# A 64-byte gap in front of the normalised activations, and a wider ring for one small tile

## The chip, the cores and the metric

The kernel runs on one core of a Trainium2 chip. The metric is the device time of one execution in microseconds, the median of several runs. Engines are called as in the profile: PE is the matrix engine (PEld its weight loads), DVE the vector engine, ACT the scalar engine, POOL the general one, SP the queue that issues most DMAs.

## The reference

Two blocks work one after the other on 512 tokens of 1024 channels in float32.

```
x = x + y @ w_out   # twice; y from hn @ w_in (1024 -> 4096): 8 heads of
                    # chunked attention, 4 heads of retention, silu gates
x = rms_norm(x)
x = x + 0.5 * swiglu(rms_norm(x))      # 1024 -> 2 x 2816 -> 1024
x = x + token_mixer(rms_norm(x))       # 1024 -> 3344 -> 1024: pooling, HGRN,
                                       # RWKV-7, gated linear attention
x = x + 0.5 * swiglu(rms_norm(x))
x = rms_norm(x)
```

Most of the arithmetic is dense products of the normalised x, or of a hidden layer, with a weight matrix.

## The kernel before

x is kept transposed, in eight tiles of 128 channels by 512 tokens. A dense product is taken in units of 128 output columns. For a unit, `wunit` loads 1024 rows by 128 columns of the weight (512 KB) into `wraw`, ACT casts them to float32r (`whi`, L188), and DVE subtracts to get the rest (`wlo`, L189). `proj_cm` then issues, for each of the eight channel tiles k, the three matmuls of `mm3`: z high by whi (L210), z low by whi (L211), z high by wlo (L212). So a unit is 24 matmuls; the stationary operand of each is a 128x128 slice of whi or wlo, the moving operand a whole 128x512 tile, and the result gathers in one bank of PSUM. Each matmul loads a new stationary slice (PEld).

The moving tiles have four names. z (z0h, z0l to z7h, z7l, made by `zsplit`) are the normalised activations, used by the projections of both layers, by the first product of both feed-forward stages, and by the mixer. h (h0h, h0l to h21h, h21l) are the hidden channels of a feed-forward stage (`ffn`): its second product takes 22 of them, 66 matmuls for each of eight output tiles. ys are the gated results of a layer, multiplied by w_out at the end of `layer`. ysh and ysl are the same for the mixer (`mix_out`). In `proj_tm` (the attention and retention values) the roles are swapped: slices of z are stationary, and slices vhi and vlo of the weight, 256 columns, move.

Every engine works through its instructions in the order of the program. Between the units stand the matmuls of attention (L456 to L480), of retention (L493 to L511), and of the mixer's recurrences; the units of the next heads are placed among those of the heads before, and in the mixer an order written out by hand (`MIX_ORDER`) does so.

SBUF is laid out by pools in the order in which they are made: persistent tiles, wp (wraw, whi, wlo, three slots each), sm (small tiles), tmp, xp (x), zp (z), and behind it the pool of the stage: b1 for the layers, ffn for a feed-forward stage, mix for the mixer. Within a pool each tile stands behind the one before, its bytes per partition rounded up to 32. All the large tiles take a multiple of 512 bytes per partition, so what sets a tile's start modulo 512 is the small tiles ahead of it. In the compiled program before, the starts modulo 512 are

```
wraw, whi, wlo            320
x, R, fa, th, z           256
b1: cosT, sinT, g, vhi, vlo                 256
b1: rtm 256 and 288; all made after rtm, ys among them   320
ffn: R and h              256
mix: ysh, ysl              32   (X, b and others 352)
```

A slice of 128 float32 of a weight tile takes 512 bytes, so each slice has the start of its tile modulo 512. The ring `rtm` (two slots of 4 float32 in 32 bytes each, made in the middle of b1) is what puts the tiles made after it 64 bytes further. The program uses SBUF up to byte 229,200 per partition.

Of the kernel before, what the change touches and what calls it, by code (L numbers as in the profile page):

```python
# [8 lines left out]
F32 = mybir.dt.float32  # L9
# [6 lines left out]
PSUM = bass.MemoryType.PSUM  # L16

T = 512
D = 1024
NT = T // 128  # L20
# [92 lines left out]
class Build:  # L113
# [36 lines left out]
    def banks(self, ctx, m, a, b, c):  # L150
        """The banks of PSUM beyond the three of psm: m more for dense products, and three pools for the rest."""
        self.mm_ring = [self.psm] * 3
        if m:
            self.mm_ring += [self.pool("psx", m, PSUM, ctx)] * m
        self.psa, self.psb, self.psc = (self.pool(n, k, PSUM, ctx) for n, k in (("psa", a), ("psb", b), ("psc", c)))
# [14 lines left out]

# [1 line left out]
    def wunit(self, src, nk=ND, dst=None):  # L172
        """128 columns of a weight as float32r high and low parts [128, nk, 128]."""
        nc = self.nc
        raw = self.wp.tile([128, 8, 128], F32, tag="wraw", name="wraw")
        nc.sync.dma_start(out=raw[:, :nk, :], in_=src.rearrange("(k p) n -> p k n", p=128))
        return self.wsplit(raw, nk, dst)
# [15 lines left out]
    def split(self, src, pool=None, tag=None, scale=None, alloc=None):  # L193
        """src (float32) times a per-partition scale, as float32r high and low parts."""
        nc = self.nc
        if alloc is None:
            alloc = lambda part: pool.tile([128, T], F32R, tag=tag + part, name=tag + part)
        hi, lo = alloc("h"), alloc("l")
        if scale is None:
            nc.scalar.copy(hi, src)  # L200
            nc.vector.tensor_tensor(out=lo, in0=src, in1=hi.bitcast(F32), op=ALU.subtract)
        else:
            nc.scalar.activation(out=hi, in_=src, func=AF.Copy, scale=scale)  # L203
            nc.vector.scalar_tensor_tensor(out=lo, in0=src, scalar=scale, in1=hi.bitcast(F32),  # L204
                                           op0=ALU.mult, op1=ALU.subtract)
        return hi, lo
# [7 lines left out]
    def proj_cm(self, src, z, order=range(ND), unit=None, bank=None):  # L214
        """128 columns of a weight, channel-major: [128 channels, tokens]."""
        hi, lo = unit or self.wunit(src)
        ps = self.mm_bank(bank)
        for i, k in enumerate(order):
            self.mm3(ps, hi[:, k, :], lo[:, k, :], z[k][0], z[k][1], i == 0, i == ND - 1)
        return ps  # L220

    def proj_tm(self, w, tt, z):
        """256 columns, token-major: [128 tokens, 256]."""
        ps = self.mm_bank()[:, :256]
        hi, lo = w
        s = slice(tt * 128, (tt + 1) * 128)
        for k in range(ND):
            self.mm3(ps, z[k][0][:, s], z[k][1][:, s], hi[:, k, :], lo[:, k, :], k == 0, k == ND - 1)
        return ps

# [1 line left out]
    def rsqrt(self, m, n, k=""):  # L232
        """m: [128, n] positive normal float32 tile; returns 1/sqrt(m)."""
        nc = self.nc
# [5 lines left out]
                                scalar2=float(0x5F3759DF), op0=ALU.mult, op1=ALU.add)  # L240
        # a step of third order, then one of Newton's
        nc.vector.tensor_tensor(out=t, in0=y, in1=y, op=ALU.mult)
# [8 lines left out]
    def sumsq_add(self, st, src, scale=None, alloc=None):  # L251
        """Adds the squares of one channel tile to the running sum of a norm."""
        nc = self.nc
        if st.get("acc") is None:
            st["acc"] = self.tmp.tile([128, T], F32, tag="nacc", name="nacc", bufs=2)
            dst = st["acc"]
        else:
            dst = alloc() if alloc else self.tmp.tile([128, T], F32, tag="nsq", name="nsq")
        kw = {} if scale is None else {"scale": scale}
        nc.scalar.activation(out=dst, in_=src, func=AF.Square, **kw)  # L260
        if dst is not st["acc"]:
            nc.vector.tensor_tensor(out=st["acc"], in0=st["acc"], in1=dst, op=ALU.add)

    def sum_tok(self, acc, n=NT):
        """Sums over channels: [128 tokens, n] from acc [128 channels, n * 128]."""
        ps = self.psc.tile([128, T], F32, tag="c", name="c")
# [11 lines left out]
    def bcast_tok(self, r, pool, tag):  # L278
        """[128 tokens, NT] to every partition: PSUM [128, T]."""
        nc = self.nc  # L280
# [10 lines left out]

# [1 line left out]
    def tables(self):  # L293
# [35 lines left out]

# [1 line left out]
    def first_block(self):  # L331
# [17 lines left out]
    def layer(self, l):  # L349
        nc = self.nc  # L350
        b1 = self.b1
        z = self.z
        w_in = self.a["w_in"]
        first = {}
# [27 lines left out]
        ahead(0, 1, (self.psa, "a"))  # L382
        rtm = b1.tile([128, NT], F32, tag="rtm", name="rtm", bufs=2)
        nc.vector.tensor_copy(out=rtm, in_=rt)
# [30 lines left out]
        def stacked(q, k):  # L415
            """The two heads apart: high and low part of q on the two halves of the rows, the high part of k on
            both, and the low part of k."""
            qs, ks = [], []
# [21 lines left out]
        def attention(p, q, k, v, g):  # L440
            """Heads 2p and 2p + 1; the result times the gate replaces the gate."""
            po = self.psc.tile([128, T], F32, tag="c", name="po")
# [73 lines left out]
        v = None  # L516
# [35 lines left out]

# [1 line left out]
    def ffn(self, w_in, w_out, first, gain=None):  # L554
# [62 lines left out]
    def last_tile(self, ps):  # L617
        """The last channels of the last residual, their squares, and the sums of all, by groups of tokens."""
        nc = self.nc
# [16 lines left out]

# [1 line left out]
    def mixer(self):  # L638
# [5 lines left out]
        with ExitStack() as ctx:  # L644
# [95 lines left out]
            def silu_of(c0, alloc, name, scale):  # L740
                """scale * silu(column group), channel-major."""
                d = scaled(c0, alloc, name, 0.5 * scale)
# [5 lines left out]
            def tokens(src, alloc, name):  # L748
                """[128 channels, tokens] to [128 tokens, NT, 128 channels]."""
                ps = self.psc.tile([128, NT, 128], F32, tag="c", name="pv")  # L750
# [42 lines left out]
    def mix_out(self, y, xs):  # L793
        """The output product of the mixer in two passes: the channels that are ready first, then the rest."""
        nc, x = self.nc, self.x
# [41 lines left out]
    def rwkv(self, e, c):  # L837
        """Heads 2c and 2c + 1: chunks of 64 tokens, two to a tile of 128."""
        nc = self.nc
# [72 lines left out]
        for tp in range(2):  # L912
# [11 lines left out]
            for h in range(2):  # L924
                for i in range(2):
# [4 lines left out]
                                        in1=mLQ.unsqueeze(1).to_broadcast([128, 2, 128]), op=mult)  # L930
        # inverse of I + L: 16 x 16 diagonal blocks by substitution, one block per partition
        scr = self.dp.tile([8, 8, 16, 16], F32, tag="scr", name="scr", bufs=2)
# [64 lines left out]

        # merges 16 -> 32 -> 64
        pst = mm8(lambda r, v, cc: zt[r, v, :], lambda r, v, cc: idq[cc], "pT")
# [13 lines left out]

        # chunk transfer matrices
        for tp in range(2):
# [35 lines left out]

        # chunk to chunk
        S = t("S", (128, 8, 64))
# [11 lines left out]

        # outputs
        bv = t("bv", (128, 8, 64))
# [43 lines left out]
    def gla_core(self, e, q, k, lf, v, finish):  # L1111
        """Gated linear attention for a pair of heads, chunks of 128 tokens: q, k, lf channel-major,
        v token-major. Within a chunk, the pairs of tokens that part at the same level of halving are
        taken in one product, with decays to and from the last token of the left half."""
        nc = self.nc
# [120 lines left out]
    def to_channels(self, on, g, gain):  # L1236
        """The token-major [128, NT, 128] on, transposed, times gain and gate, into the gate's tile."""
        nc = self.nc
# [55 lines left out]
    def hgrn(self, e):  # L1294
# [3 lines left out]
        V = e["V"]  # L1298
        # lower bounds: softmax over the one layer, cumulated, minus the first
        lb = e["small"]("lb", 2)  # L1300
# [96 lines left out]
    def finish(self):  # L1397
        """The last norm, token-major: the channels of x times their gains are transposed, and the tokens scaled
        on the way out of PSUM."""
        nc = self.nc  # L1400
# [16 lines left out]
    def run(self):  # L1417
        nc = self.nc
        self.setup()
        self.zp = self.pool("zp")  # L1420
        self.dp = self.pool("dp", 1, bass.MemoryType.DRAM)
        self.fg = self.pers.tile([128, 8], F32, name="fg")
# [61 lines left out]
```

## Time and profile before

| | before |
|---|---|
| median of 3 runs | 1720.46 us (1719.25 to 1720.58) |
| the profiled execution, from its first to its last instruction | 1720.4 us |
| PE busy | 1695.1 us, 9648 matmuls |
| DVE busy | 987.0 us |
| ACT busy | 628.9 us |
| mean granted clock of PE | 0.989 |

The profiled execution's span is within 0.1 us of the median, so the span and the time can be read as one. A matmul's recorded duration runs on past the start of the next one, since matmuls are pipelined; what a matmul costs in a dense stretch is the distance from its start to the next one's start.

### The profile page before, as it was taken

Reading aid. Unit: us, or ns where it says so; the run is one execution under the profiler, and the core shown is the slowest. Engines: PE = TensorE matmul, PEld = TensorE weight load, DVE = VectorE, ACT = ScalarE, POOL = GpSimd, SP = SyncE. Lnnn points to the kernel's source line nnn. Section 1 sums busy time; section 2 is a strip of 40 time slices with the busy share of each in tenths; the row PEclk is TensorE's granted clock in tenths of the full one; section 3 lists DMA queues with packets and bytes.
Section 4 is the critical chain, followed back from the end, with each engine's and each line's share of the span. In section 5 each row is a group of like instructions: output and inputs, shape, how many; then the busy total and the mean of one; then the engine's idle time right before and its main releaser. Section 6 shows DMA issues by size and latency. Waiting matters only on the chain.

```text
span 1720.4 us, 24093 instructions
## 1 busy us (share of the span) xinstructions
PE 1695.1 (99%) x9648; PEld 1335.9 (78%) x9648; DVE 987.0 (57%) x1972; ACT 628.9 (37%) x1077; POOL 62.4 (4%) x58
## 2 busy tenths in 40 slices
PE   8999999999999999999999999999989999999998
PEld 6777788777778888888888877777767888888886
DVE  7684756554465675554433377658868654454222
ACT  6553323454332432232222235327435332222221
POOL 0001110000111000000000100000200000000000
PEclk9999999999999999999999999989989999999999
DMA  7221223422122223333333432212013323333331
GB/s 239 83 84 38 81 61 92 135 80 80 38 81 64 76 84 100 93 91 98 95 101 108 124 87 66 54 38 59 24 48 96 114 88 98 99 88 90 101 92 59
DMA packets 270673, 147.33 MB, mean 86 GB/s; under 512 B 10576, under 2 KB 264288, under 8 KB 270560
## 3 DMA queue, kind: packets, MB, share of 16 engines
q1 hardware_dynamic: 265600, 140.40, 28.0%
q0 software_dynamic: 1280, 4.20, 0.8%
q8 instruction: 76, 1.25, 0.3%
q10 hardware_dynamic: 3680, 1.19, 0.3%
q14 instruction: 37, 0.30, 0.1%
HBM read 141.30 MB, written 4.46 MB: 85 GB/s over the span
## 4 chain that ended last, share of the span: by engine, by line
PE 92%; DVE 4%; ACT 2%; DMA 1%; issue 1%; SPq 0%; DVEq 0%; ACTq 0%
PE mm L212 26%; PE mm L211 26%; PE mm L210 26%; PE po L480 2%; PE pt L472 1%; PE s L457 1%; PE po L498 1%; PE s L493 1%; PE s L456 1%; DMA wraw<-in_w_in 1%; PE pO L1084 1%; PE pO L1082 1%; DVE xr L1187 0%; PE po L1231 0%; DVE wlo L189 0%
## 5 line engine op out<-in xcount | busy, mean ns | idle before, releaser
L188 ACT CAST whi<-wraw 128x1024 fp32r<-128x1024 f32 (+2 forms) x244 | 244.7, 1004 | 716.7 <-PE mm L211 496.0
L189 DVE TENSOR_TENSOR wlo<-wraw,whi 128x1024 fp32r<-128x1024 f32 (+2 forms) x244 | 287.1, 1179 | 156.9 <-ACT whi L188 156.3
L593 DVE SCALAR_TENSOR_TENSOR fa<-mm,R 128x512 f32<-128x512 f32 x44 | 30.4, 692 | 114.8 <-PE mm L212 114.8
L589 DVE SCALAR_TENSOR_TENSOR fa<-mm,R 128x512 f32<-128x512 f32 x44 | 30.3, 691 | 96.5 <-PE mm L212 95.3
L210 PE MATMUL mm<-z0h,whi 128*128 128x512 f32 x163 | 68.4, 420 | 6.1 <-ACT z0h L203 5.7
L211 PE MATMUL mm<-z7l,whi 128*128 128x512 f32 x163 | 65.8, 404 | 0.9 <-DVE z7l L204 0.9
L212 PE MATMUL mm<-z0h,wlo 128*128 128x512 f32 x163 | 66.2, 406 | 0.0
L211 PE MATMUL mm<-z0l,whi 128*128 128x512 f32 x163 | 66.2, 406 | 0.0
L210 PE MATMUL mm<-z6h,whi 128*128 128x512 f32 x163 | 66.0, 405 | 0.0
L210 PE MATMUL mm<-z4h,whi 128*128 128x512 f32 x163 | 65.9, 405 | 0.0
L212 PE MATMUL mm<-z6h,wlo 128*128 128x512 f32 x163 | 65.9, 404 | 0.0
L211 PE MATMUL mm<-z3l,whi 128*128 128x512 f32 x163 | 65.8, 403 | 0.0
L210 PE MATMUL mm<-z7h,whi 128*128 128x512 f32 x163 | 65.3, 401 | 0.3 <-ACT z7h L203 0.3
L210 PE MATMUL mm<-z5h,whi 128*128 128x512 f32 x163 | 65.6, 402 | 0.0
L212 PE MATMUL mm<-z3h,wlo 128*128 128x512 f32 x163 | 65.5, 402 | 0.0
L211 PE MATMUL mm<-z5l,whi 128*128 128x512 f32 x163 | 65.5, 402 | 0.0
L211 PE MATMUL mm<-z6l,whi 128*128 128x512 f32 x163 | 65.3, 401 | 0.0
L211 PE MATMUL mm<-z4l,whi 128*128 128x512 f32 x163 | 65.3, 401 | 0.0
L212 PE MATMUL mm<-z4h,wlo 128*128 128x512 f32 x163 | 65.3, 401 | 0.0
L210 PE MATMUL mm<-z2h,whi 128*128 128x512 f32 x163 | 65.3, 400 | 0.0
L211 PE MATMUL mm<-z2l,whi 128*128 128x512 f32 x163 | 65.2, 400 | 0.0
L212 PE MATMUL mm<-z1h,wlo 128*128 128x512 f32 x163 | 65.2, 400 | 0.0
(737 smaller groups left out, 4241.4 us busy)
## 6 DMA issues: line engine op xcount, KB each, us to landing
wraw<-in_w_in SPq DMA_DIRECT2D x90, 512.0 KB, 4.0
wraw<-in_ffn_w_in SPq DMA_DIRECT2D x88, 512.0 KB, 3.7
wraw<-in_ffn_w_out SPq DMA_DIRECT2D x32, 512.0 KB, 3.9
wraw<-in_w_out SPq DMA_DIRECT2D x16, 512.0 KB, 4.2
wraw<-in_ffn_w_out SPq DMA_DIRECT2D x16, 384.0 KB, 3.5
bias<-in_relb SPq DMA_DIRECT2D x16, 256.0 KB, 2.8
x<-in_xT SPq DMA_DIRECT2D x8, 256.0 KB, 5.3
decay<-in_decay SPq DMA_DIRECT2D x8, 256.0 KB, 2.9
```

The costliest lines, as they stand in the source:

```text
L188: nc.scalar.copy(hi[:, ks, :], raw[:, ks, :])
L189: nc.vector.tensor_tensor(out=lo[:, ks, :], in0=raw[:, ks, :], in1=hi[:, ks, :].bitcast(F32), op=ALU.subtract)
L210: mm(out, lhsT=lh, rhs=rh, start=start, stop=False)
L211: mm(out, lhsT=lh, rhs=rl, start=False, stop=False)
L212: mm(out, lhsT=ll, rhs=rh, start=False, stop=stop)
L456: nc.tensor.matmul(ps, lhsT=qt, rhs=k[0][h][:, :n], start=True, stop=False)
L457: nc.tensor.matmul(ps, lhsT=qt[hr], rhs=k[1][hr, :n], start=False, stop=True)
L472: nc.tensor.transpose(pt[:, ks], s[:, ks], self.ident)
L480: nc.tensor.matmul(po[64 * h:64 * h + 64, t * 128:(t + 1) * 128], lhsT=v[:, kt, vc:vc + 64], rhs=pts[h][:, ks], start=(kt == 0), stop=(kt ...
L493: nc.tensor.matmul(ps, lhsT=k[:, kt * 128:(kt + 1) * 128], rhs=q[:, T - n:], start=True, stop=True)
L589: nc.vector.scalar_tensor_tensor(out=a2, in0=pg, scalar=0.5, in1=R, op0=ALU.mult, op1=ALU.mult)
L593: nc.vector.scalar_tensor_tensor(out=a2, in0=pu, scalar=0.5, in1=R, op0=ALU.mult, op1=ALU.mult)
```

## The change

A tile of 128 partitions by 16 float32 (64 bytes per partition) is made as the first tile of zp and set to zero by POOL. It is never read. z and all pools behind it start 64 bytes further. The ring rtm takes tiles of 64 float32 (256 bytes) in place of 4, of which the first four columns are used as before; its two slots take 512 bytes in place of 64. So all tiles of b1 made after rtm stand 512 bytes further, which leaves their starts modulo 512 as they were. Docstrings and comments are dropped without a change of line numbers.

```diff
-        rtm = b1.tile([128, NT], F32, tag="rtm", name="rtm", bufs=2)
+        rtm = b1.tile([128, 64], F32, tag="rtm", name="rtm", bufs=2)[:, :NT]
...
         self.zp = self.pool("zp")
+        gap = self.zp.tile([128, 16], F32, name="gap")
+        nc.gpsimd.memset(gap, 0.0)
         self.dp = self.pool("dp", 1, bass.MemoryType.DRAM)
```

After it, z, h, vhi and vlo start at 320 modulo 512, ysh and ysl at 96, and ys and the weights at 320 as before.

## Rows read from the trace of the kernel before

**Rows 1.** The page: span; busy time by engine; PE and its clock in 40 slices.

```profile
span 1720.4 us, 24093 instructions
PE 1695.1 (99%) x9648; PEld 1335.9 (78%) x9648; DVE 987.0 (57%) x1972; ACT 628.9 (37%) x1077; POOL 62.4 (4%) x58
...
PE   8999999999999999999999999999989999999998
...
PEclk9999999999999999999999999989989999999999
```

**Rows 2.** The chain of work that ended last, shares of the span.

```profile
PE 92%; DVE 4%; ACT 2%; DMA 1%; issue 1%; SPq 0%; DVEq 0%; ACTq 0%
PE mm L212 26%; PE mm L211 26%; PE mm L210 26%; PE po L480 2%; PE pt L472 1%; PE s L457 1%; PE po L498 1%; PE s L493 1%; PE s L456 1%; DMA wraw<-in_w_in 1%; PE pO L1084 1%; PE pO L1082 1%; DVE xr L1187 0%; PE po L1231 0%; DVE wlo L189 0%
```

**Rows 3.** PE's waits, longest in total first: us, times, longest.

```profile
PE mm L210 <- ACT z0h L203: 5.7, 1, 5.7
PE mm L210 <- ACT ysh L200: 4.3, 1, 4.3
PE psc L1210 <- DVE xr L1187: 2.0, 4, 0.8
```

**Rows 4.** Busy time by stretch: layer 1, layer 2, feed-forward, mixer, feed-forward.

```profile
20.00:286.00 266.00, 265.49 (x1456) 209.03 (x1455) 173.91 (x408) 109.99 (x229) 20.63 (x10) 1.00 0.29 83
...
330.00:560.00 230.00, 229.83 (x1279) 180.52 (x1277) 129.16 (x311) 92.31 (x194) 19.75 (x10) 1.00 0.24 70
...
606.00:870.00 264.00, 264.00 (x1150) 213.20 (x1149) 141.40 (x203) 78.57 (x98) 0.00 (x0) 1.00 0.31 91
...
1000.00:1300.00 300.00, 291.61 (x2894) 217.47 (x2892) 224.96 (x561) 133.35 (x260) 12.40 (x18) 0.94 0.18 49
...
1350.00:1590.00 240.00, 239.99 (x1033) 192.22 (x1032) 122.53 (x158) 70.77 (x88) 0.00 (x0) 1.00 0.32 94
```

**Rows 5.** Matmuls on z0h, one of each unit: all, then 1352 to 1585 us.

```profile
L210 PE MATMUL mm<-z0h,whi x163: 390/398/796, 5.7 to 1578.0; 128*128 128x512 f32 x163
...
L210 PE MATMUL mm<-z0h,whi x41: 394/394/394, 1354.0 to 1578.0; 128*128 128x512 f32 x41
```

**Rows 6.** Matmuls on h0h: all, then 850 to 1010 us.

```profile
L210 PE MATMUL mm<-h0h,whi x16: 394/396/398, 860.5 to 1691.4; 128*128 128x512 f32 x16
...
L210 PE MATMUL mm<-h0h,whi x8: 398/398/398, 860.5 to 968.3; 128*128 128x512 f32 x8
```

**Rows 7.** Matmuls on ys, 286 to 335 us; first and last by wlo in the timeline.

```profile
L212 PE MATMUL mm<-ys,wlo x35: 389/389/389, 286.3 to 309.4; 128*128 128x512 f32 x35
...
286.28 0.39 PE L212 MATMUL mm<-ys,wlo 128*128 128x512 f32 x1
...
309.40 0.39 PE L212 MATMUL mm<-ys,wlo 128*128 128x512 f32 x1
```

**Rows 8.** Timeline of PE on ysh and ysl, first and last of 21 matmuls.

```profile
1309.81 0.40 PE L212 MATMUL mm<-ysh,wlo 128*128 128x512 f32 x1
...
1314.48 0.40 PE L212 MATMUL mm<-ysh,wlo 128*128 128x512 f32 x1
```

**Rows 9.** The 256-column matmuls on z0h, 40 to 51.5 us.

```profile
L210 PE MATMUL mm<-vhi,z0h x4: 281/283/283, 40.1 to 48.7; 128*128 128x256 f32 x4
```

**Rows 10.** DVE's and ACT's groups by shape, 1352 to 1585 us; the last, 1180 to 1260 us.

```profile
L188 ACT CAST whi<-wraw 128x1024 fp32r<-128x1024 f32 x41 | 43.0, 1049 | 144.8 <-issue 76.1 <-PE mm L211 65.0 <-PE mm L212 3.6
...
L189 DVE TENSOR_TENSOR wlo<-wraw,whi 128x1024 fp32r<-128x1024 f32 x41 | 50.1, 1222 | 4.3 <-ACT whi L188 4.3
...
L594 DVE TENSOR_TENSOR fa<-fa,th 128x512 f32<-128x512 f32 x21 | 14.5, 692 | 0.7
L201 DVE TENSOR_TENSOR h0l<-fa,h0h 128x512 fp32r<-128x512 f32 x1 | 0.7, 693 | 0.1
...
L1179 DVE TENSOR_TENSOR X<-b 128x512 f32<-128x512 f32 x12 | 7.8, 687 | 0.2
```

**Rows 11.** Attention of the first layer: the timeline; busy time of two stretches.

```profile
64.71 0.43 PE L480 MATMUL po<-pT,v 128*64 128x128 f32 x2
...
65.50 0.44 PE L472 MATMUL pt<-cst,s 128*128 128x128 f32 x2
...
65.70 0.48 PE L210 MATMUL mm<-z4h,whi 128*128 128x512 f32 x1
...
62.00:74.00 12.00, 11.94 (x67) 7.15 (x65) 8.80 (x33) 6.43 (x18) 0.00 (x0) 1.00 0.25 73
75.00:100.00 25.00, 25.00 (x158) 22.15 (x154) 23.79 (x42) 9.20 (x14) 0.00 (x0) 1.00 0.15 43
```

**Rows 12.** POOL's largest memset and its last instruction of the first 60 us.

```profile
L711 POOL MEMSET sc<- 128x1024 f32 x2 | 1.9, 976 | 0.0
...
0.35 0.10 POOL L1475 MEMSET const-uint8-127<- 128x1 uint8 x1
```

## The prediction

> **What bounds the kernel now.** I read the page first. PE is busy for 1695.1 of 1720.4 us and runs at nearly its full clock throughout [rows 1]. The chain of work that ended last agrees: 92% of it is PE, and 78% is the three matmuls of the dense products alone [rows 2]. PE's recorded waits are few; the two largest, 5.7 us at the start and 4.3 us in the mixer, are 10 us together [rows 3]. The table by stretch says where PE has slack: none in the feed-forward stretches (264.00 of 264.00 and 239.99 of 240.00 us), half a microsecond in a layer, and 8.4 of 300 us in the mixer [rows 4]. So what counts is the distance between the starts of two dense matmuls. A busy engine doesn't tell that distance, and neither do the recorded durations of 390 ns or so, because they overlap.
>
> I worked the distance out for each kind of moving tile.
>
> - z: in the second feed-forward stage, z0h comes once in each unit of 24 matmuls, 41 times, from 1354.0 to 1578.0 us. That is 224.0 us for 40 x 24 = 960 matmuls: 233.3 ns [rows 5].
> - h: h0h comes 8 times, once in 66 matmuls, from 860.5 to 968.3 us. 107.8 us for 462 matmuls: 233.3 ns [rows 6].
> - ysh and ysl: 20 steps from 1309.81 to 1314.48 us: 233.5 ns [rows 8].
> - ys: the 35 matmuls by wlo, one in three, go from 286.28 to 309.40 us. 23.12 us for 102 steps: 226.7 ns [rows 7].
>
> All four kinds have the same shape, 128x512 on a fresh 128x128 stationary slice, at the full clock. One kind is 6.6 ns (2.8%) faster. By the table of starts in the section on the kernel, ys is also the only kind whose tile starts where the weights do modulo 512 (320 and 320). z and h start 64 bytes before the weights, ysh and ysl 288 before. Two different unequal distances give the same 233.3 to 233.5 ns, so equality and not nearness seems to matter. That reading is the ground of the forecast: the kernel before already holds a trial of the change.
>
> **The change part by part.**
>
> The gap moves z and h from 256 to 320, so their matmuls become pairs of equal starts, as those of ys are. There are 163 units on z [rows 5], 163 x 24 = 3912 matmuls; and 16 columns on h [rows 6], 16 x 66 = 1056. Together 4968. Each goes from 233.3 to 226.7 ns: 4968 x 6.65 ns (233.33 less 226.68) = 33.0 us. Bounds for one matmul: nothing, if the start is not the cause (first rival), and 6.65 ns, the only two rates that the rows show. I take 6.65, since ys is the same instruction with the same operands' starts.
>
> Where the gain can be lost. In the feed-forward stages nothing else is near. A unit would take 24 x 226.7 = 5.44 us in place of 5.60; for each, DVE's subtraction takes 1.22 us and ACT's cast 1.05 [rows 10], and both engines are busy for about half of these stretches or less [rows 4]. The DMAs there move 91 to 94 GB/s, which would become some 94 to 97; in the first layer's stretch around w_out the trace has ys running at 226.7 ns without a wait [rows 7]. So the feed-forward matmuls, 2 x 44 x 24 = 2112 on z and all 1056 on h, give their full 21.1 us.
>
> The layers and the mixer have the other 163 - 88 = 75 units, 1800 matmuls, worth 12.0 us. Some of these stand among matmuls that wait for a chain through DVE and ACT. At 64.71 us two products start, the next transposes start at 65.50, and the dense matmul after them at 65.70: PE had nothing to issue for some tenths of a microsecond although it counts as busy, and two dense matmuls less 13 ns change nothing there [rows 11]. From 75 to 100 us DVE is busy for 23.79 of 25 us, so the softmax behind it can come late [rows 11]. In the mixer PE's share is 97% and DVE's 75% [rows 4]. The loss lies between nothing and the whole 12.0 us. The nearest row for the bulk is that of the layers' stretches, where PE is idle for 0.7 of 496 us; most dense matmuls there run in whole units, not among the attention. I take a quarter: 3 us lost. What is late next at these places is the softmax on DVE and ACT, and in the mixer DVE's products of the gated attention.
>
> The wider rtm keeps all tiles of b1 behind it, ys, qs, ks, s, pT and v among them, at 320. If the gap came alone they would move to 384, and ys would leave the weights; with it they stay, for nothing. Bound: 384 matmuls on ys (two layers, 8 x 24 each) by 6.65 ns, 2.6 us, were they to change.
>
> vhi and vlo move with z, from 256 to 320, and remain equal to their stationary partner. Their step is (48.7 - 40.1) / 72 = 119 ns [rows 9]. I take no change. Were the place itself and not the equality to matter, their 768 matmuls could change by 6.65 ns each either way: 5.1 us.
>
> ysh and ysl go from 32 to 96, still unequal: no change, at most a gain of 192 x 6.65 ns = 1.3 us.
>
> The memset of the gap is one instruction at the head of POOL's queue. The largest memset in the trace, 64 times as wide, takes 0.98 us, and POOL has nothing to do from 0.45 us to beyond 60 us [rows 12]; nobody reads the gap. Cost 0 for that cover; without it, under 1 us.
>
> DVE and ACT write z and h, and read and write the mixer's tiles, at other starts than before. The sums of two tiles take 692 ns with all three at 256 (fa, th), 693 with h0l at 256, and 687 with X and b at 352 [rows 10]: no effect of the start that would count.
>
> **The sum.** 1720.4 - 33.0 + 3.0 = 1690.4 us. The span stands within 0.1 us of the median of the runs, so this is the time too.
>
> The Trainium skill, in "TensorE: Matmul & The Clock Gate", section "Part 2: What happens when you issue a matmul", speaks against the change: PE has two independent read ports, and loading the next stationary tile takes nothing from the running matmul's reads. By that rule no placement of the two tiles could matter, and the sum would be 1720.4 us. This trace doesn't agree, as far as 226.7 against 233.3 ns shows it.
>
> **The rivals.**
>
> *The starts are not the cause.* The ys stretch could be faster for another reason: another mix of work beside it (one cast and one subtraction per unit, no tanh and fewer products of DVE), or its place high in SBUF. Against it: h lies in the same part of SBUF as ys, and the h stretches have as little beside them as the ys stretch, yet they keep 233.3 ns to the tenth. For it: only one stage shows the fast rate. Then the time is 1720.4 us, no change. The rule named above would give this too. Chance 0.07.
>
> *The feed-forward gains, the rest is lost.* All dense matmuls get faster, but the chains in the layers and the mixer set their length. 1720.4 - 21.1 = 1699.3 us, and with some new waits up to 1710. For it: DVE at 95% for 25 us and the waits in rows 11. Against it: PE's idle time in the layers is a fifth of a percent. Chance 0.10, most of it below 1702.
>
> *Equal starts cost, and ys is fast for its own reason.* The 256-column pairs are equal already and take 119 ns for 256 columns, 0.47 ns a column, more than z's 0.456. If the price of a column were theirs, a dense matmul would take 238 to 240 ns, and 4968 x 5 to 6 ns make 25 to 30 us: about 1748 us. It decides as soon as a dense matmul on z passes 233.3 ns. Against it: ys again, equal and 0.443 ns a column; the short pairs rather have a fixed part that counts double per column. Chance 0.03.
>
> **How the numbers follow.** The forecast, 1690.4 us, has a chance of 0.80. Its own range goes from 1684 (no loss, 1687.4, and the side effects of vhi and ysh in part) to 1699 (the second rival's sum). The range that is to hold 8 in 10 reaches to 1702, into the second rival. About 0.2% (3.4 us) is what a measurement of this kernel can tell from no change. Faster by more: 0.80 and 0.10, 0.90. Within it: 0.07. Slower: 0.03.
>
> **What would show it.** In the changed kernel's profile, the steps of z0h in the second feed-forward stage and of h0h should be 24 x and 66 x 226.7 ns (5.44 and 14.96 us). ys should stay at 226.7, ysh at 233 to 234, the 256-column pairs at 119 ns. The feed-forward stretches should end 21 us earlier in all, the layers and the mixer some 9. PE's waits should grow only around the softmax and in the mixer. The prediction is wrong if z stays at 233 ns, if h and z part, or if DVE or ACT take longer for the same shapes.

## The result, and the profile after

The changed kernel takes 1695.45 us in the median of four runs (1694.79 to 1697.89), against 1720.52 us before. The ratio is 0.9854, with a 95% interval from 0.9841 to 0.9866: faster by 25.1 us. The forecast was 1690.4 us, the range 1684 to 1702.

The page of the profile after, to set beside [rows 1]. The profiled execution is the slowest of the four, 1697.89 us by its own time, and its span is 24.3 us shorter than before. In this run the span is 1.8 us below the time, so the two can't be read as one, as I had read them before; below, spans are compared with spans and times with times.

```profile
span 1696.1 us, 24094 instructions
PE 1669.0 (98%) x9648; PEld 1337.3 (79%) x9648; DVE 986.6 (58%) x1972; ACT 628.9 (37%) x1077; POOL 62.8 (4%) x59
...
PEclk9999999999999999999999999989979999999999
```

DVE, ACT and POOL are as busy as before, with one instruction more on POOL. PE has the same matmuls and is busy for 26.1 us less.

The rows by tile for z0h (second feed-forward stage), h0h, ys and the 256-column matmuls after, with the first and the last start in the second column of times, as in [rows 5 to 7, 9]:

```profile
L210 PE MATMUL mm<-z0h,whi x41: 389/389/389, 1339.9 to 1557.5; 128*128 128x512 f32 x41
...
L210 PE MATMUL mm<-h0h,whi x8: 389/389/389, 849.8 to 954.5; 128*128 128x512 f32 x8
...
L212 PE MATMUL mm<-ys,wlo x37: 389/389/389, 282.9 to 307.4; 128*128 128x512 f32 x37
...
L210 PE MATMUL mm<-vhi,z0h x4: 278/283/283, 39.5 to 48.1; 128*128 128x256 f32 x4
```

z: 217.6 us for 960 matmuls, 226.7 ns, where it was 233.3. h: 104.7 us for 462, 226.6 ns, where it was 233.3. ys: 24.5 us for 108, 226.9 ns, as before within the rounding of the row (this row counts 37 matmuls, two more than that of before). The 256-column matmuls: 8.6 us for 72, 119 ns, as before.

Where did the 24.3 us of the two profiles come from? I cut both at starts of z0h and h0h, which every unit has once. The layers are cut at the fourth and the 49th z0h, the mixer at the 96th and the 120th, and the last stage at the last h0h. The "all matmuls at 226.7" column is the number of dense matmuls on z and h in the stretch by 6.65 ns.

```
stretch                     before    after   shorter by   all matmuls at 226.7
layers (45 units on z)       582.4    578.9       3.5            7.2
first feed-forward           373.4    363.0      10.4           10.5
head of the mixer             18.9     18.6       0.3            0.5
mixer (24 units on z)        332.5    333.2      -0.7            3.8
second feed-forward          356.3    346.3      10.0           10.1
```

The feed-forward stages gave all that was in them. In these two profiles the layers gave about half and the mixer nothing. The rows show the ends of the layers' and of the mixer's stretch, first before (with the mixer by busy time and clock), then after:

```profile
L210 PE MATMUL mm<-z0h,whi x46: 390/398/692, 27.9 to 610.4; 128*128 128x512 f32 x46
...
L210 PE MATMUL mm<-z0h,whi x25: 391/397/505, 1002.7 to 1335.1; 128*128 128x512 f32 x25
...
1002.70:1335.10 332.40, 323.57 (x3097) 242.09 (x3096) 253.89 (x618) 151.09 (x290) 13.50 (x20) 0.95 0.20 56
```

```profile
L210 PE MATMUL mm<-z0h,whi x46: 389/396/687, 27.6 to 606.5; 128*128 128x512 f32 x46
...
L210 PE MATMUL mm<-z0h,whi x25: 389/396/628, 988.1 to 1321.3; 128*128 128x512 f32 x25
```

PE's longest waits after (compare [rows 3]), and the mixer by busy time and clock:

```profile
PE mm L210 <- ACT z0h L203: 5.7, 1, 5.7
PE mm L210 <- ACT ysh L200: 4.3, 1, 4.3
PE psc L1210 <- DVE xr L1187: 2.1, 4, 0.8
...
988.10:1321.30 333.20, 323.17 (x3097) 242.51 (x3096) 253.81 (x618) 150.98 (x290) 13.63 (x20) 0.95 0.20 56
```

The three longest waits have hardly grown, so the loss is not in any of them. Nor did PE stand longer at 1.2 GHz, the lower of its two levels, in the mixer: it was 34.1 us before and 34.1 us after. What differs is which matmuls fell into that time, 31 dense steps on z after and 21 before, and at 427 ns a step that makes some 2 us.

One more thing stands in the timeline of PE. It shows the first dense matmuls behind eight short products, in the first layer:

```profile
33.94 0.48 PE L210 MATMUL mm<-z0h,whi 128*128 128x512 f32 x1
34.26 0.39 PE L211 MATMUL mm<-z0l,whi 128*128 128x512 f32 x1
34.49 0.39 PE L212 MATMUL mm<-z0h,wlo 128*128 128x512 f32 x1
34.72 0.40 PE L210 MATMUL mm<-z1h,whi 128*128 128x512 f32 x1
34.95 0.39 PE L211 MATMUL mm<-z1l,whi 128*128 128x512 f32 x1
35.18 0.40 PE L212 MATMUL mm<-z1h,wlo 128*128 128x512 f32 x1
35.41 0.39 PE L210 MATMUL mm<-z2h,whi 128*128 128x512 f32 x1
```

From 34.26 to 35.41 us five steps take 230 ns or a little more, not 226.7. A run of dense matmuls reaches the fast rate only after some steps. Between the cuts of the layers, 194 of the 902 steps from a z matmul to the next dense one (those under 245 ns) take 230 ns or more; in the mixer it is 160 of 393.

### The profile page after: what moved, and what is told of

Read it like the earlier page. It is cut to its first block, busy times and chain, and to the rows that moved or that the text cites. A ratio compares the mean times of both kernels' runs of the same rounds, so it can differ in the third digit from the quotient of the medians.

```text
span 1696.1 us, 24094 instructions
## 1 busy us (share of the span) xinstructions
PE 1669.0 (98%) x9648; PEld 1337.3 (79%) x9648; DVE 986.6 (58%) x1972; ACT 628.9 (37%) x1077; POOL 62.8 (4%) x59
## 4 chain that ended last, share of the span: by engine, by line
PE 90%; DVE 6%; ACT 2%; DMA 1%; issue 1%; SPq 0%; DVEq 0%; ACTq 0%; POOLq 0%
PE mm L211 25%; PE mm L212 25%; PE mm L210 25%; PE po L480 2%; PE pt L472 1%; PE s L457 1%; PE po L498 1%; PE s L493 1%; PE s L456 1%; DMA wraw<-in_w_in 1%; DVE wlo L189 1%; PE pO L1084 1%; PE pO L1082 1%; DVE xr L1187 0%; PE bc L286 0%
## 5 line engine op out<-in xcount | busy, mean ns | idle before, releaser
L593 DVE SCALAR_TENSOR_TENSOR fa<-mm,R 128x512 f32<-128x512 f32 x44 | 30.3, 691 | 107.8 <-PE mm L212 107.8
```

Of the source, the lines that this page charges most:

```text
L593: nc.vector.scalar_tensor_tensor(out=a2, in0=pu, scalar=0.5, in1=R, op0=ALU.mult, op1=ALU.mult)
```

## The experiments

Three questions were open. Is it the equality of the starts, or the place 320? Is 512 the modulus? Where did the missing 4.9 us (25.1 against the forecast 30.0) go? Times are given with the ratio to the kernel before on the same chip; that kernel took 1721.5 to 1722.8 us there.

**Bare matmuls at twelve distances** (m1). Stationary slices and moving tiles in the kernel's pattern, the moving tile's start moved by g bytes against the stationary slice's. `unit(p, g, 2)` issues 48 dense matmuls; the second loop makes runs of 24 behind four short products.

```diff
+        for g in (0,) + GAPS:
+            p = bank(f"d{g}e")
+            unit(p, g, 2)
...
+        for g in (0, 448):
+            for r in range(4):
...
+            unit(p, g, 2, cols=256)
```

> A kernel of matmuls alone, 128x512 float32r in the kernel's pattern of three, 48 matmuls for each distance in bytes of the moving tile's start behind the stationary slice's: 0, 16, 32, 64, 128, 192, 256, 320, 384, 448, 480, 496. It computes nothing of the reference. Equality theory: 226.7 ns from start to start at distance 0, 233 to 234 at all others. If nearness or a coarser modulus counts, 256 or 16 and 496 also come to 227. If the starts are not the cause, one rate for all. Then runs of 24 behind four short float32 products, with no other engine in the way: if the loss in the layers and the mixer comes from waits for DVE and ACT, all of the 24 take 226.7 ns at distance 0 here; if a run begins at the slow rate by itself, the first 5 to 15 take 233 to 236 ns here too. At 448 all 24 take 233. Stationary slices by turns at equal start and 64 bytes behind: between the rates, or 233 throughout. 256 columns: 119 to 120 ns at distance 0; at 448 6.7 ns more if the price is one for each matmul, 3.3 if it goes by column.

Rows by tile of this kernel, one matmul in three, 16 to a group; the name holds the distance:

```profile
L49 PE MATMUL d64e<-zh,whi x16: 388/388/399, 59.0 to 69.4; 128*128 128x512 f32 x16
...
L49 PE MATMUL d256e<-zh,whi x16: 389/389/398, 92.4 to 102.6; 128*128 128x512 f32 x16
...
L49 PE MATMUL d448e<-zh,whi x16: 394/394/394, 125.5 to 136.0; 128*128 128x512 f32 x16
...
L49 PE MATMUL half0e<-zh,whi x16: 277/283/283, 221.5 to 226.9; 128*128 128x256 f32 x16
...
L49 PE MATMUL half448e<-zh,whi x16: 276/276/286, 227.2 to 232.4; 128*128 128x256 f32 x16
```

Settled, in the mean of the last 24, the steps are 226.7 ns at 0 and at 256, 228.9 at 64 and 320, 231.7 at 16, 232.1 and 232.3 at 128 and 384, and 233.3 at 32, 192, 448, 480 and 496. So the distance does set the rate, with no other work on the core but one sum for each bank. Equality modulo 512 is too strict: 256 is as good. The 256-column matmuls hold a surprise: 120.0 ns at distance 0 and 113.3 at 448. For them equal starts are the slow case. By column the best of both shapes is the same, 0.443 ns (226.7 for 512, 113.3 for 256).

With stationary slices by turns at the equal start and 64 bytes behind, the steps repeat as 226, 226, 236 and 232 ns, 230.0 in the mean: between the rates.

The runs behind short products begin slow here too. In one at distance 0 the steps are 318, 231, 236, 228, 233 and 231 ns, and 226.7 from the seventh on; in another 314, 233, 230 and then 226.7. At distance 448 they stay at 233.3 in the mean. No other engine is in the way here, so this is PE's own.

**Everything shifted, the distances kept** (e1). The kernel before, with 64 bytes ahead of the weights.

```diff
         self.ones = p.tile([128, 128], F32, name="ones")
+        shift = p.tile([128, 16], F32, name="shift")
+        nc.gpsimd.memset(shift, 0.0)
```

> The kernel before with a 64-byte tile ahead of the weight pool: weights 384, z and h 320, ys 384 modulo 512. Equality theory: z and h stay at 233.3 ns, ys at 226.7, the time is that of before, 1720 us within 3. Place theory (320 is a good start for a moving tile): z and h 226.7, ys 233, about 1696 to 1698 us.

1721.76 us, ratio 0.9999 (0.9990 to 1.0008). In this kernel's rows by tile, h0h takes 107.8 us for 462 matmuls, 233.3 ns, though it starts at 320; ys at 384 keeps 23.1 us for 102, 226.5 ns:

```profile
L212 PE MATMUL mm<-h0h,whi x8: 398/398/398, 859.8 to 967.6; 128*128 128x512 f32 x8
...
L212 PE MATMUL mm<-ys,whi x35: 389/389/389, 285.8 to 308.9; 128*128 128x512 f32 x35
...
L212 PE MATMUL mm<-z0h,whi x25: 392/397/505, 1001.9 to 1336.9; 128*128 128x512 f32 x25
```

The place theory is out. It is the distance. (The mixer takes 335.0 us in this profile, from the 96th to the 120th z0h, against 332.5 in that of before, although z has the same distance in both. This is how far two profiles of the mixer can lie apart.)

**The gap without the wider rtm** (e2).

```diff
-        rtm = b1.tile([128, 64], F32, tag="rtm", name="rtm", bufs=2)[:, :NT]
+        rtm = b1.tile([128, NT], F32, tag="rtm", name="rtm", bufs=2)
```

> The change without the wider rtm: z, h and the weights at 320, ys at 384. Equality theory: z and h 226.7, ys 233.3; 384 matmuls by 6.65 ns are 2.6 us, less what runs begin slow anyway: 1697 to 1698 us against 1695.5 for the whole change. If ys has a reason of its own, ys stays at 226.7 and the time is that of the change.

1696.33 us, ratio 0.9848 (0.9832 to 0.9865); the time can't be told from the change's. The rows of ys can:

```profile
L211 PE MATMUL mm<-ys,whi x35: 394/394/394, 283.8 to 307.2; 128*128 128x512 f32 x35
```

23.4 us for 102 steps, 229.4 ns. That is neither of the two rates that I had, but it is near the map's value for 64 bytes behind, 228.9. So rtm keeps 384 matmuls some 2.7 ns faster, about 1 us, not 2.6.

**The mixer's last product too** (e3). The mixer's small tiles go behind its large ones, which puts ysh and ysl at 320.

```diff
+            ms = self.pool("mixs", 1, ctx=ctx)
...
-                return mp.tile([128, n], F32, tag=name, name=name)
+                return ms.tile([128, n], F32, tag=name, name=name)
```

(lm and selrk likewise.)

> The change, and in the mixer the small tiles (lm, sel, om, w0h, a0h, oka, selrk and those of the same helper) go to a pool of their own behind the mixer's, so that ysh and ysl start at 320 as the weights do. Equality theory: ysh 226.7 in the long runs, 192 matmuls by 6.65 ns are 1.3 us, about 1694.3 us. If the distance doesn't matter, 1695.5.

1695.28 us, ratio 0.9839 (0.9825 to 0.9854). The interval takes in the change's, so the time settles nothing; e5 below shows the rate.

**A finer map and runs of several lengths** (m2). As m1, 36 matmuls at every eighth byte, and runs of n dense matmuls between four short products.

```diff
+        for g in range(0, 512, 8):
+            block(f"d{g}e", g, 36)
+        for g in range(0, 512, 16):
+            block(f"half{g}e", g, 48, 256)
+        for n in (1, 2, 3, 6, 12, 24):
+            for g in (0, 448):
```

> Matmuls alone again; nothing of the reference is computed. 36 matmuls of 128x512 for each distance from 0 to 504 bytes in steps of 8, 48 of 128x256 in steps of 16, and runs of 1, 2, 3, 6, 12 and 24 dense matmuls with four short float32 products between the runs, at distances 0 and 448. Modulo-256 theory: the map from 256 on repeats the one below; 226.7 ns at 0 and 256 alone, 229 at 64 and 320, else 231 to 234. Modulo-512 theory with 256 by chance: no repetition elsewhere. For 256 columns: 120 at 0, 113 at most others if the order is reversed there, and again a period of 256. Runs: if a run's beginning is slow by itself, the gain of distance 0 over 448 is under 1 ns for each matmul in runs of 1 to 3, 3 to 4 ns in runs of 6 to 12 and 5 to 6 in runs of 24. If only waits for other engines cost gain in the kernel, it is 6.65 ns in all run lengths here.

Steps worked from the trace, in ns, mean of the last 24 of each distance; for the runs, the mean distance from one group of short products to the next, at 448 less at 0, by the number of dense matmuls between them. From 256 on the table repeats to 0.1 ns, so half of it stands here:

```
512 columns, distance 0 to 248 by 8:
  0: 226.7 233.3 231.7 233.5 233.3 233.3 233.3 230.0
 64: 228.9 235.6 231.1 233.3 233.3 230.0 231.1 240.0
128: 232.1 233.3 233.3 233.5 234.4 233.3 233.3 233.3
192: 233.3 233.3 234.6 234.4 233.3 233.3 236.7 230.0
256 columns, distance 0 to 240 by 16:
  0: 120.0 118.8 116.7 118.3 117.8 120.0 120.0 113.3
128: 118.5 118.8 117.3 119.3 113.3 119.2 118.3 117.3
gain of distance 0 over 448 for each matmul, in runs of
  1: 6.6    2: 5.0    3: 1.1    6: 3.8    12: 4.4    24: 5.6
```

Rows of three distances, one matmul in three, so 33 steps from the first start to the last (at 256 with some slow steps at the beginning):

```profile
L60 PE MATMUL d8e<-zl,whi x12: 398/398/398, 45.5 to 53.2; 128*128 128x512 f32 x12
...
L60 PE MATMUL d120e<-zl,whi x12: 400/403/403, 162.3 to 170.2; 128*128 128x512 f32 x12
...
L60 PE MATMUL d256e<-zl,whi x12: 389/389/397, 305.4 to 312.9; 128*128 128x512 f32 x12
```

The modulus is 256. For 512 columns only 0 gives 226.7; 8 bytes behind already cost all of it, 8 bytes before (248) half of it, and 120 behind (240.0) are worse than the old 64 before. The runs of 6, 12 and 24 came out about as I had written, 3.8, 4.4 and 5.6 ns of the 6.6. The short ones did not: a single matmul gains the whole step, two gain 5.0 each, and three only 1.1. Part of the loss in the layers and the mixer, where dense matmuls often stand in short runs, is therefore PE's own.

**The change again, and the values apart** (c1, e4, e5). Since 256-column matmuls want other distances, vhi and vlo get a gap of 192 bytes, and the narrow rtm takes ys to 256 bytes from equality. e5 is e4 with the edit of e3.

```diff
             self.sinT = b1.tile([128, T], F32, name="sinT")
+            vgap = b1.tile([128, 48], F32, name="vgap")
+            nc.gpsimd.memset(vgap, 0.0)
...
-        rtm = b1.tile([128, 64], F32, tag="rtm", name="rtm", bufs=2)[:, :NT]
+        rtm = b1.tile([128, NT], F32, tag="rtm", name="rtm", bufs=2)
```

> The change itself, as a base for the next two on the same chip: 1695 to 1698 us, 0.985 of before.

> The change, but a gap of 192 bytes ahead of vhi and vlo and the narrow rtm: vhi and vlo at 0 and ys at 64 modulo 512, z and the weights at 320. Theory that 256-column matmuls pay for equal starts: 768 matmuls go from 120 to 113.3 ns, 5.1 us less than the change: 1690.3. If the map of the bare matmuls doesn't carry over to the kernel, 120 ns stay and the time is the change's. ys, now 256 bytes from equality: 226.7 ns by the modulo-256 theory, 229 to 234 by the modulo-512 one, which would cost 1 to 2.6 us.

> The same with the mixer's small tiles moved behind, so that ysh and ysl are at 320 too: another 0.5 to 1.3 us less, 1689 to 1690 us.

On one chip the change takes 1696.35 us (ratio 0.9847, 0.9833 to 0.9860), e4 1694.34 (0.9835, 0.9821 to 0.9848) and e5 1693.31 (0.9830, 0.9816 to 0.9843). Rows of e4, then two lines of e5's timeline on ysh, 19 steps apart:

```profile
L212 PE MATMUL mm<-ys,wlo x35: 389/389/389, 283.7 to 306.8; 128*128 128x512 f32 x35
...
L210 PE MATMUL mm<-vhi,z0h x4: 281/281/281, 39.5 to 47.9; 128*128 128x256 f32 x4
```

```profile
1291.68 0.39 PE L210 MATMUL mm<-ysh,whi 128*128 128x512 f32 x1
...
1295.98 0.39 PE L212 MATMUL mm<-ysh,wlo 128*128 128x512 f32 x1
```

ys, 256 bytes from equality, has 226.5 ns: modulo 256 holds in the kernel. ysh in a long run has 226.3 ns in place of 233.5. The values went from 119.9 ns to 117.8 in the mean of all their steps, not to 113.3: 1.6 us gained of 5.1. So both versions miss what I had written, 1690.3 and 1689 to 1690 us. e5 is still the best version found, 3.0 us under the change in the medians of this chip, though the intervals of their ratios overlap.

**The values on the other side** (e8). e5 with vhi and vlo 64 behind z modulo 256:

```diff
-            vgap = b1.tile([128, 48], F32, name="vgap")
+            vgap = b1.tile([128, 16], F32, name="vgap")
...
-        rtm = b1.tile([128, NT], F32, tag="rtm", name="rtm", bufs=2)
+        rtm = b1.tile([128, 24], F32, tag="rtm", name="rtm", bufs=2)[:, :NT]
```

> As the version with ysh too, with vhi and vlo 64 bytes behind z modulo 256 in place of 64 before it (128 against 64). In the bare matmuls 64 before gave 113.3 ns and 64 behind 117.8, yet in the kernel 64 before gave 117.8. If the roles' sign is what differs, 64 behind gives 113.3 in the kernel: 768 x 4.5 ns, 3.4 us less than the version before, some 1690 us. If the map depends on more than the distance, anything from 113 to 120 ns.

1694.78 us, ratio 0.9841 (0.9827 to 0.9856), and again 117.8 ns. The sign is not what differs. Of the three distances that the kernel tried for 256 columns, two agree with the bare map, 0 (119.9 against 120.0) and 64 behind (117.8 both). Only 64 before does not, 117.8 against 113.3, and why stays open.

**Less and more work for PE, in the mixer and in the layers** (e6, e9, e7). One of a unit's 24 matmuls is left out, or issued twice:

```diff
-        mm(out, lhsT=lh, rhs=rl, start=False, stop=False)
+        if not skip:
+            mm(out, lhsT=lh, rhs=rl, start=False, stop=False)
...
+                     skip=self.lean and k == 3)
```

In e9 `for _ in range(2 if skip else 1):` stands in place of the `if`. `lean` is set around the mixer (e6, e9) or around a layer's units (e7).

> The change, leaving out one of the 24 matmuls (the low part of the fourth channel tile) in each of the mixer's 27 units on z, 27 x 226.7 ns = 6.1 us of PE work, more than the 4.3 us that the faster rate was worth there. If the mixer's length is set by chains through DVE and ACT, its stretch from the 96th z0h to the 120th keeps 332 to 334 us and the time stays within 2 us of the change's. If the mixer kept the old length because its short runs of dense matmuls begin slow, it gets 5 to 6 us shorter.

> The opposite of the run that left matmuls out: the change, issuing the matmul of the low part of the fourth channel tile twice in each of the mixer's 27 units on z (the result counts that small product double), 27 x 226.7 ns = 6.1 us more PE work. If the mixer's length followed PE, 6 us more, some 1702 us. If it is set by chains alone, no change, 1696. If the granted clock is what the run with less work paid for, more dense work raises the clock in the mixer above 0.95 and the time comes out at or below the change's in spite of the added work.

> The change, leaving out the same matmul in 47 units on z of the two layers: 47 x 226.7 ns = 10.7 us of PE work. If the layers' length follows PE, and their missing gain of 2 to 3 us comes from slow beginnings of runs, the layers' stretch gets 9 to 11 us shorter. If chains swallow part of what PE saves there, in the measure in which the gain fell short (5 of 7 us arrived), 6 to 8.

e6, with 6.1 us less for PE, takes 1702.52 us (0.9891, 0.9876 to 0.9906): longer. e9, with 6.1 us more, takes 1702.62 us (0.9889, 0.9872 to 0.9905). The mixer's stretch, by the ends of z0h and by busy time, in the change (c1), in e6 and in e9:

```profile
L210 PE MATMUL mm<-z0h,whi x25: 389/397/501, 985.9 to 1319.7; 128*128 128x512 f32 x25
...
985.90:1319.70 333.80, 322.38 (x3098) 242.31 (x3097) 253.51 (x618) 151.03 (x291) 13.65 (x20) 0.95 0.20 56
```

```profile
L212 PE MATMUL mm<-z0h,whi x25: 387/397/767, 986.3 to 1322.9; 128*128 128x512 f32 x25
...
986.30:1322.90 336.60, 322.36 (x3074) 242.54 (x3073) 255.08 (x619) 145.03 (x287) 14.04 (x22) 0.92 0.21 57
```

```profile
L212 PE MATMUL mm<-z0h,whi x25: 388/397/506, 986.4 to 1326.3; 128*128 128x512 f32 x25
...
986.00:1327.00 341.00, 331.25 (x3127) 250.14 (x3125) 255.24 (x619) 150.94 (x291) 13.37 (x20) 0.94 0.20 55
```

333.8, 336.6 and 339.9 us. 24 units lie between the cuts, so 5.4 us of PE's work are gone in e6 and added in e9. Neither of the two lengths written for e6, 332 to 334 us or 5 to 6 less, came out.

In e6 PE is busy for as long as in the change, 322.4 us, although 24 matmuls are gone, and it is idle for 14.2 us in place of 11.4. The granted clock accounts for the first: the mean fell from 0.95 to 0.92, and PE stood at 1.2 GHz for 51.2 us of the stretch, busy for 45.7 of them, in place of 34.1 and 33.9. At that level a dense step takes 427 ns in place of 227, so the 11.8 us more of busy time there cost an estimated 5.5 us, as much as was taken out. The other 2.8 us are idle time, that is, waits. Two rows of e6 show the largest of these drops, and that PE was busy all the time before it:

```profile
1085.00:1105.00 20.00, 20.00 (x226) 14.25 (x225) 7.70 (x22) 2.46 (x6) 0.00 (x0) 1.00 0.19 54
1105.00:1119.00 14.00, 14.00 (x67) 10.88 (x67) 3.09 (x19) 1.04 (x1) 0.00 (x0) 0.51 0.01 1
```

e9 is 6.1 us longer, some more than was added, and it too stood longer at 1.2 GHz, for 41.0 us. It doesn't show the higher clock that the third expectation asked for. So neither run shows what PE's work is worth in the mixer at an unchanged clock. They show that the time at the lower level changes with the work and can eat all that was saved.

e7, with 10.7 us less for PE in the layers, takes 1687.54 us (0.9802, 0.9786 to 0.9819). Its z0h go from 26.7 to 595.1 us; those of the change from 27.6 to 604.3:

```profile
L212 PE MATMUL mm<-z0h,whi x46: 387/396/687, 26.7 to 595.1; 128*128 128x512 f32 x46
```

```profile
L210 PE MATMUL mm<-z0h,whi x46: 389/396/687, 27.6 to 604.3; 128*128 128x512 f32 x46
```

568.4 against 576.7 us: 8.3 of the 10.2 us (45 units) that were taken out of this stretch, four fifths. That lies between the two theories. The layers mostly follow PE, and about a fifth of what it saves doesn't arrive; that waits swallow it is the likely reading, not shown by this run alone.

## Why the prediction was right, and what was off

**The rate.** 226.7 ns for z and h was forecast, and 226.7 and 226.6 came. The reading of the trace before, that ys was a trial of the change, is confirmed: m1 and m2 show the distance alone making the rate, and e1 shows that the place doesn't. The rule of the Trainium skill that I had set against it ("TensorE: Matmul & The Clock Gate", "Part 2: What happens when you issue a matmul"), by which loading a stationary tile takes nothing from a running matmul's reads, would allow no such dependence on placement; the runs have it, 226.7 against 233.3 ns in bare matmuls that differ in the distance alone.

**The modulus.** I took 512 from the sizes of the tiles. It is 256 (m1, m2, and ys in e4). For this change both give the same answer, which is luck: no moving tile of the kernel before stood 256 bytes from the weights, and one that did would have been told wrongly.

**The sum.** The term of 33.0 us stands for the rate; the feed-forward stages delivered 20.4 of the 20.6 us that lay between their cuts. The term that was mis-sized is the loss in the layers and the mixer. I took a quarter of 12.0 us, 3 us. By the medians it is 33.0 - 25.1 = 7.9 us.

- *The layers* gave 3.5 of 7.2 us in the profile after, and 5.7 in that of the repeated run (c1). The difference is one unit, the first of the second layer: 7.3 us before, 7.6 after, 5.5 in c1. PE waits in it for z7h and z7l from ACT and DVE, 1.2 us before, 1.6 after and not at all in c1; why they come late is open. Outside this unit both profiles gain 3.8 of the 7.0 us that were there. PE's matmuls come in the same order in all these profiles, so they can be compared step by step. The 880 steps from dense to dense gain 4.6 us of 5.9 (4.5 in c1): a run of dense matmuls begins at the slow rate, which is new to me and which m1 and m2 show with PE alone. The first steps of runs, behind a short product, gain 0.1 of 0.5. The last ones, before another product, take 0.3 us more in place of 0.7 less, and all other matmuls take 0.5 to 0.6 us more. That these last two are waits for DVE and ACT is argued, not shown; that a fifth of what e7 saves doesn't arrive fits it.
- *The mixer* gave nothing of its 3.8 us in these two profiles. I had read its PE share of 97% as room for a gain [rows 4]. About 390 steps from dense to dense at the full clock gain 1.5 of 2.6 us, and the rest of the stretch takes more than that back. But a single profile of the mixer says little: with z's old distances it takes 332.5 and 335.0 us (before, e1), with the new ones 332.0 to 333.7 in eight profiles. So the gain lies between nothing and 3 us. What takes it stays open. In the profile after, 2 us went to the ten dense steps more that fell into the time at 1.2 GHz; in c1 there were 21 of them as before, and one wait before a short product took 2.3 us in place of 0.5. e6, in which the clock moved, doesn't settle it.

**The wider rtm.** It does keep ys fast, as I said. Without it ys falls to 229.4 ns, not to 233.3: 64 behind is not 64 before (e2).

**vhi, vlo, the memset, DVE and ACT.** All came out at no change, as forecast. That equal starts can cost was my third rival, and I set it aside for dense matmuls rightly. But the row it leaned on, 119 ns for 256 columns, meant something: those matmuls do pay for equal starts, as m1 shows (120.0 against 113.3 ns). I had explained the 119 ns by a fixed part that counts double by column. That was wrong: at the best distance 256 columns take just half of what 512 take.

**The rivals.** The second, where the feed-forward stages gain and the rest is lost (1699.3 us), and the forecast with its quarter lost (1690.4) lie on both sides of the result. The rival's time was not reached, but its effect is there: about half of the gain in the layers is lost, and most or all of that in the mixer. Its mechanism, chains through DVE and ACT, is only a part of it, since in the layers the slow beginnings of runs take about as much as what may be put down to chains.

## What to carry to other kernels

Look at the distance from start to start for each pair of tiles, not at busy shares or recorded durations: one stage that runs the same instruction faster than the others is a free trial. Where stationary slices are reloaded for every matmul, lay the moving and the stationary tile out on purpose, and try distances modulo 256 for each shape by itself, since 512 columns want 0 and 256 columns don't. Count the gain in full only where long runs of such matmuls set the time; in stretches of short runs and of chains, leave some work out first, see whether the stretch gets shorter at all, and read the granted clock beside it, since less work can change that too. Take more than one profile of a stretch before a microsecond of it is explained.

## What the runs showed of the hardware that was not expected

- The rate has a period of 256 bytes in the distance, is not symmetric (64 behind 228.9 ns, 64 before 233.3; 8 behind 233.3, 8 before 230.0), and has worse places than the old one: 240.0 ns at 120 bytes.
- For 256 columns the order is reversed in bare matmuls: 120.0 ns at distance 0, 113.3 at 112 and 192. In the kernel 64 to either side gave 117.8, of which 64 behind agrees with the bare matmuls and 64 before (113.3 there) does not.
- At distance 0 a run behind short products takes up to eleven steps in these traces, at 224 to 241 ns, most of them over 230, before it settles at 226.7. At 448 it stays at 233.3 in the mean.
- With less work for PE in the mixer, the mean granted clock there fell from 0.95 to 0.92, 51.2 us at 1.2 GHz in place of 34.1, and the kernel got longer, 1702.5 against 1696.4 us.
